# Strided attention of group A: queries and keys copied by ScalarE into neighbouring columns

## The chip, the core and the metric

The kernel runs on one core of a Trainium2 chip. The core has TensorE (PE in the profile, with PEld for its loads of stationary operands), VectorE (DVE), ScalarE (ACT), GpSimd (POOL) and SyncE (SP, which issues the DMAs here). Each engine works through its own instructions in the order in which they were written; semaphores order the engines among each other. The metric is device time in microseconds (us) of one launch, the median of several runs.

## What is computed

One decoder layer over 2048 tokens of width 1024. One projection feeds four groups of four heads (A to D), each with its own kind of attention, and a last projection `w_out` adds the gated outputs to the input. The change is in group A, dilated attention: each head attends three times with 128 queries to a block, with token strides 1, 4 and 16, and the three results are merged by their softmax denominators.

```python
DILATED_CONFIGS = ((128, 1), (512, 4), (2048, 16))

def dilated_attention(q, k, v, table_h):
    b, nh, s, dh = q.shape
    outs, lses = [], []
    for window, rate in DILATED_CONFIGS:
        fold = lambda t: t.reshape(b, nh, s // rate, rate, dh).transpose(0, 3, 1, 2, 4).reshape(b * rate, nh, s // rate, dh)
        o, lse = banded_attention(fold(q), fold(k), fold(v), table_h, window // rate, dist_scale=rate)
        ...
    wts = jax.nn.softmax(jnp.stack(lses, axis=0), axis=0)
    return jnp.sum(wts[..., None] * jnp.stack(outs, axis=0), axis=0).astype(q.dtype)
```

With stride 16 each of the 16 residue classes has 128 tokens, one block, so a block of queries sees its own block of keys alone. With stride 4 each of the 4 classes has 4 blocks, and a block sees its own and the one before it, except the first.

## The kernel before

The program goes through groups C, D, then A and B together, and the output projection. A Python planner writes it: it keeps a clock of its own for each engine (`T`), adds an estimated duration at each operation (`op`), and issues next whatever its clocks call ready. What comes out is one fixed order for each engine; on the chip nothing is reordered.

`group_ab` has 48 units of group A and 16 of group B. Units 0 to 31 are the strided ones (`make_a`, list `ORDER`): for each head four units of stride 16, then four of stride 4, each with four query blocks. Units 32 to 47 are the stride-1 units (`make_a1`), which alternate with the 16 units of group B (`make_b`). A unit runs like this:

- scores (`a_unit`, L1639): two matmuls a query block, since keys come as a rounded part and a remainder; eight a unit, into two PSUM tiles `s`. In a stride-16 unit all move 128 columns; in a stride-4 unit two move 128 and six 256.
- VectorE adds the bias and takes the row maximum (L1644, L1649); ScalarE takes exp and row sums (L1655).
- PE turns the weights (L393), ScalarE copies them rounded (`ph`, L399), VectorE makes the remainder (`pl`, L403), PE multiplies with the values (L422), ScalarE takes the result out of PSUM (`ot`, L371), PE turns it back (L435), and VectorE alone (L439) or ScalarE and VectorE (L442, L444) add its halves.

A head's queries and keys lie in SBUF by token: 2048 neighbouring columns of 4 bytes, in `wb` for even heads, in `AQ` and `keys` for odd ones. Before the change the strided units let the matmuls pick every 4th or 16th column, both for the stationary operand (queries) and for the moving one (keys). `make_a`'s `setup` also loads the next head, the bias rows and, at the end of the strided units, the first tiles of the stride-1 units (`a_more`) and of group B (`b_more`).

When nothing of a unit is ready for PE, the planner takes a step of the output projection (`out_proj`; three matmuls of 512 columns at L2148). 24 such matmuls are one job, a block of 128 rows, with one tanh (L2096) and one rounding copy (L2116) on ScalarE, four turns on PE (L2112), and on VectorE one product (L2100), one remainder (L2122) and two additions (L2154). The first 16 jobs (384 matmuls) need groups C and D; the other 16 need A and B of their rows, so the first of them waits for the first four stride-1 units.

## Time and profile before

| | us |
|---|---|
| median of 3 runs | 1802.55 (1792.04 to 1805.48) |
| the profiled execution, its own time | 1795.48 |
| its span, first to last instruction | 1793.7 |
| PE busy | 1721.8 (96%) |
| VectorE busy | 1330.1 (74%) |
| ScalarE busy | 1073.2 (60%) |

The profile is of one execution. Busy shares are means over stages with different limits; a PE that counts as busy need not run at its peak, since a matmul's end is modelled. In the trace the strided scores run from 1364.8 to 1504.5 us, the stride-1 units and group B up to about 1743 us, and then only output projection is left. The granted TensorE clock was 0.984 of full speed over the span.

### The profile page before, as it was taken

What the parts mean: (1) busy time and instruction counts of PE and PEld (TensorE: products, weight loads), DVE (VectorE), ACT (ScalarE), POOL (GpSimd) and SP (SyncE); (2) the same over time, 40 slices, a digit from 0 to 9 for tenths busy, and PEclk for the clock granted to TensorE, in tenths of its full rate; (3) what the DMA queues carried; (4) which work ended last, traced back from release to release, by engine and by line L of the source; (5) the groups of instructions that cost most, each with busy time, mean ns of one, the idle gap of its engine ahead of it and who ended that gap; (6) DMA issues with size and microseconds to landing.
All of it is one profiled execution on the core that took longest, in us unless ns stands there. A gap on an engine that the chain in (4) does not pass through costs nothing.

```text
span 1793.7 us, 31779 instructions
## 1 busy us (share of the span) xinstructions
PE 1721.8 (96%) x10035; PEld 1507.1 (84%) x10035; DVE 1330.1 (74%) x4072; ACT 1073.2 (60%) x2588; POOL 688.6 (38%) x841
## 2 busy tenths in 40 slices
PE   7989999999998999899989999999989999899999
PEld 5878878788787888789878789999869999788987
DVE  5446778998899996688476778887166777788873
ACT  4345556666675764567466566776256776467651
POOL 4666563544453654112344532223511121433231
PEclk9999999999999999999988999999999999999999
DMA  7763555334446325731484422323375768999986
GB/s 243 232 206 108 173 169 165 99 115 140 115 141 195 113 79 163 202 119 66 135 271 142 149 64 85 118 56 95 121 226 173 228 202 268 284 309 324 298 262 221
DMA packets 283480, 308.24 MB, mean 172 GB/s; under 512 B 80256, under 2 KB 201216, under 8 KB 282640
## 3 DMA queue, kind: packets, MB, share of 16 engines
q1 hardware_dynamic: 283312, 306.21, 55.5%
q8 instruction: 80, 1.31, 0.3%
q14 instruction: 88, 0.72, 0.1%
HBM read 219.47 MB, written 86.92 MB: 171 GB/s over the span
## 4 chain that ended last, share of the span: by engine, by line
PE 49%; DVE 3%; DMA 2%; issue 1%; POOL 1%; SPq 1%; ACT 1%; DVEq 0%; ACTq 0%; POOLq 0%
PE j L833 12%; PE o L422 9%; PE j L2148 8%; PE pt L393 7%; PE s L943 4%; PE s L1639 4%; PE pt L435 2%; PE s L1329 1%; PE s L1428 1%; SPq L156 1%; PE pt L2112 1%; PE s L1941 1%; DVE pl L403 0%; DMA BQ<-tqB 0%; DVE prow L945 0%
## 5 line engine op out<-in xcount | busy, mean ns | idle before, releaser
L833 PE MATMUL j<-wb,xh 128*128 128x512 f32 (+2 forms) x2048 | 619.6, 383 | 12.8 <-ACT wb L618 7.8
L833 PEld LDWEIGHTS j<-wb,xh 128*128 128x128 f32 x2048 | 372.2, 191 | 59.2 <-POOL xh L571 7.7
L833 PE MATMUL j<-wb,xl 128*128 128x512 f32 (+2 forms) x1024 | 386.4, 377 | 0.9 <-POOL xl L577 0.9
L399 ACT ACTIVATE ph<-pt 128x512 fp32r<-128x512 f32 (+4 forms) x486 | 265.4, 575 | 128.2 <-PE pt L393 121.3
L403 DVE TENSOR_TENSOR pl<-pt,ph 128x512 fp32r<-128x512 f32 (+4 forms) x486 | 311.4, 658 | 37.4 <-ACT ph L399 37.0
L833 PEld LDWEIGHTS j<-wb,xl 128*128 128x128 f32 x1024 | 194.6, 190 | 27.2 <-POOL xl L577 2.2
L679 POOL TENSOR_TENSOR ss<-ss,expo 128x6 f32<-128x6 f32 (+2 forms) x64 | 117.1, 1830 | 214.2 <-DVE ss L677 202.9
L577 POOL TENSOR_TENSOR xl<-xt,xh 128x512 fp32r<-128x512 f32 x112 | 150.1, 1340 | 9.3
L371 ACT ACTIVATE ot<-o 128x512 f32<-128x512 f32 (+1 forms) x160 | 81.5, 509 | 101.2 <-PE o L422 100.7
L943 PE MATMUL s<-keys,Q 128*128 128x512 f32 (+3 forms) x320 | 113.1, 400 | 11.8 <-DVE mx L945 6.9
L571 POOL TENSOR_SCALAR xh<-xt 128x512 fp32r<-128x512 f32 x128 | 84.5, 660 | 76.7 <-DMA xt<-in_xt_dram 48.0
L2102 POOL TENSOR_TENSOR xt<-xt,sq 128x512 f32<-128x512 f32 x32 | 41.6, 1299 | 184.6 <-DVE sq L2100 58.4
L660 ACT ACTIVATE stqk<-j 128x512 f32<-128x512 f32 x64 | 38.3, 598 | 122.8 <-PE j L833 122.7
L945 DVE CUSTOM_DVE_ANT_0 prow<-s,Hs 128x512 f32<-128x512 f32 (+3 forms) x160 | 94.3, 605 | 20.8 <-PE s L943 14.2
L674 DVE TENSOR_REDUCE ss<-sq 128x6 f32<-128x384 f32 (+2 forms) x64 | 39.4, 615 | 93.7 <-ACT sq L664 93.5
L1059 DVE SCALAR_TENSOR_TENSOR pa<-pb,ra,pa 128x1024 f32<-128x1024 f32 (+4 forms) x96 | 104.2, 1112 | 2.3
L945 DVE CUSTOM_DVE_ANT_0 pa<-s,H 128x512 f32<-128x512 f32 (+3 forms) x160 | 93.6, 604 | 14.1 <-PE s L943 12.1
L1655 ACT ACTIVATE ap<-ap,AO 128x128 f32<-128x128 f32 (+1 forms) x192 | 86.4, 454 | 24.0 <-DVE AO L1649 23.8
L945 DVE CUSTOM_DVE_ANT_0 pb<-s,H 128x512 f32<-128x512 f32 (+3 forms) x160 | 92.8, 603 | 4.1 <-PE s L943 3.2
L435 PE MATMUL pt<-ident,ot 128*128 128x128 f32 x512 | 86.7, 283 | 4.0 <-DVE pl L403 2.0
L1043 ACT ACTIVATE pa<-pa,nm 128x128 f32<-128x128 f32 (+7 forms) x64 | 76.9, 1202 | 22.1 <-DVE nm L951 21.7
L1523 ACT ACTIVATE prow<-prow,nm 128x128 f32<-128x128 f32 (+7 forms) x64 | 76.9, 1202 | 17.5 <-DVE nm L951 16.5
(265 smaller groups left out, 4206.3 us busy)
## 6 DMA issues: line engine op xcount, KB each, us to landing
xt<-in_xt_dram SPq DMA_DIRECT2D x128, 256.0 KB, 3.5
xr<-in_x_dram SPq DMA_DIRECT2D x16, 512.0 KB, 5.6
Q<-tqC SPq DMA_DIRECT2D x64, 128.0 KB, 3.3
DQ<-tqD SPq DMA_DIRECT2D x16, 512.0 KB, 4.8
raw<-gate_d SPq DMA_DIRECT2D x32, 256.0 KB, 4.4
stqk<-in_x_dram SPq DMA_DIRECT2D x32, 256.0 KB, 5.0
acc_d<-stqk SPq DMA_DIRECT2D x32, 256.0 KB, 4.4
stqk<-acc_d SPq DMA_DIRECT2D x32, 256.0 KB, 4.3
```

The costliest lines, as they stand in the source:

```text
L393: PE.transpose(ps[:rows, x * 128:(x + 1) * 128], src(), ident)
L399: A.activation(ph[:rows, :n], ps[:rows, :n], AF.Copy)
L403: V.tensor_tensor(pl[:rows, :n], ps[:rows, :n], ph[:rows, :n], op=OP.subtract)
L422: PE.matmul(u["po"][:, c0:c0 + wd], lhsT=lhsT(), rhs=x[:rows, col:col + wd], start=u["k"] == 1, stop=u["k"] == total, skip_group_check=True)
L435: PE.transpose(ps[:, i * 128:(i + 1) * 128], ot[:, i * 128:(i + 1) * 128], ident)
L577: G.tensor_tensor(l, xt, h, op=OP.subtract)
L679: G.tensor_tensor(ss[:, :nh], ss[:, :nh], expo[:, :nh], op=OP.pow)
L833: PE.matmul(ps[:, :n], lhsT=xx[:, ks], rhs=W[k][ww][:, lo:hi], start=(k == 0 and i == 0), stop=(k == KT - 1 and i == 2))
L943: PE.matmul(ps[:, :n], lhsT=q(), rhs=k[:, k0:k0 + n], start=(i == 0), stop=(i == np_ - 1))
L945: V.tensor_tensor_reduce(st["row"][:, k0:k0 + n], ps[:, :n], rev(H, t * 128 + 127 - k0, n), 1.0, LOW, OP.add, OP.max, st["mx"][:, ci:ci + 1])
L1059: V.scalar_tensor_tensor(rows[i][:, k0:k0 + n], part[i][:, k0:k0 + n], ra[:, 1:2], rows[i][:, k0:k0 + n], op0=OP.mult, op1=OP.add)
L2148: PE.matmul(ps, lhsT=xx[:, ks], rhs=OW[half, (k, c)][ww], start=(x == 0 and k == 0 and i == 0), stop=(x == len(halves) - 1 and k == 3 and ...
```

## The change

Two new tiles `AC`, each 128 partitions by 3 times 512 columns, are used in turn by the strided units. A new function `gather(n)` lets ScalarE copy a unit's 512 queries into the first third of its tile, in neighbouring columns; for stride 4 two more copies bring its 512 keys (rounded part and remainder) into the other thirds. The copies still read every 4th or 16th column. Stride-16 units keep reading their keys in place, with stride. The copies of unit n+1 are put off to 3 us (of the planner's clock) after unit n's setup, and a unit's scores wait for its own copies (`cready`). In all there are 16 + 16 * 3 = 64 copies of 128x512.

Three things go with it: the planner no longer counts strided scores as slower than others; the third part of the `AC` tiles takes the place of group B's query tile `BQ`, and the first two parts that of the last two tiles of output weights (`ow`); so `b_more`, which loads group B's first two units, moves from the setup of unit 28 to that of unit 32.

```diff
                     for x in range(2):
                         PE.matmul(ps[:, s0:s0 + n], lhsT=qs(j), rhs=ks(x, j, prevs[j]), start=(x == 0), stop=(x == 1))
-                        e = op("PE", mm(n) if r == 1 else max(217.0, 0.92 * n)) + 60.0
+                        e = op("PE", mm(n)) + 60.0
...
+        AC = [as_.tile([128, 3, 512], F32R, name="AC%d" % i) for i in range(2)]
+        cready = {}
+
+        def gather(n):
+            h, r, q0 = ORDER[n]
+            Q, K = QK[h % 2]
+            C = AC[n % 2]
+            for i, src in enumerate((Q,) if r == 16 else (Q, K[:, 0], K[:, 1])):
+                src = src.rearrange("p (c r) -> p r c", r=r)
+                if r == 16:
+                    A.activation(C[:, i].rearrange("p (j c) -> p j c", j=4), src[:, q0:q0 + 4], AF.Copy)
+                else:
+                    A.activation(C[:, i], src[:, q0 // 4], AF.Copy)
+                cready[n] = op("ACT", av(512), aready[h])
...
+                if n == 0:
+                    defer(aready[0], lambda: gather(0))
+                if n + 1 < len(ORDER):
+                    defer(max(T["PE"] + 3000.0, aready.get(ORDER[n + 1][0], 0.0)), lambda: gather(n + 1))
...
-                if n == len(ORDER) - 4:
-                    b_more()
...
             def source():
-                Q, K = QK[h % 2]
-
-                def cols(j, i0, n):
-                    rho, i = divmod(q0 + j, nb)
-                    c0 = rho + r * 128 * (i - i0)
-                    return slice(c0, c0 + (n - 1) * r + 1, r)
-                return (lambda j: Q[:, cols(j, 0, 128)]), (lambda x, j, p: K[:, x, cols(j, p, 128 * (1 + p))]), Hs[h, r]
+                C, K = AC[n % 2], QK[h % 2][1]
+                if r == 16:
+                    ks = lambda x, j, p: K[:, x, q0 + j::r]
+                else:
+                    ks = lambda x, j, p: C[:, 1 + x, (j - p) * 128:(j + 1) * 128]
+                return (lambda j: C[:, 0, j * 128:(j + 1) * 128]), ks, Hs[h, r]
...
-            u = a_unit(r, q0, setup, room, lambda: max(at("s"), aready[h]), source,
+            u = a_unit(r, q0, setup, room, lambda: max(at("s"), cready.get(n, INF)), source,
...
-                    parts += [as_.tile([128, 1024], F32R, name="ow%d" % i) for i in range(2)]
+                    parts += [t[:, 0:2].rearrange("p i c -> p (i c)") for t in AC]
+                    b_more()
...
-            Qb = as_.tile([128, 2, 256], F32R, name="BQ", bufs=2)
+            Qb = AC[hd[1] % 2][:, 2].rearrange("p (j c) -> p j c", j=2)
```

How the order moves, at three places. The first is ScalarE in the stride-4 units of head 0 (units 4 to 7). Before (`ap` are the weights, `pt` turned weights, `o` a unit's result):

```order
L1655 ACTIVATE ap,AO<-ap,AO 128x128
L1655 ACTIVATE ap,AO<-ap,AO 128x256
L399 ACTIVATE ph<-pt 128x512
L1655 ACTIVATE ap,AO<-ap,AO 128x256 x2
L371 ACTIVATE ot<-o 128x512
L1655 ACTIVATE ap,AO<-ap,AO 128x128
L1655 ACTIVATE ap,AO<-ap,AO 128x256
L399 ACTIVATE ph<-pt 128x384
```

ScalarE at the same place in the changed kernel; the lines below the change stand 16 to 18 higher in its file, so L2114 is the tanh of L2096:

```order
L1695 ACTIVATE AC_17188<-wb 128x512 x3
L1655 ACTIVATE ap,AO<-ap,AO 128x128
L1655 ACTIVATE ap,AO<-ap,AO 128x256
L399 ACTIVATE ph<-pt 128x512
L1655 ACTIVATE ap,AO<-ap,AO 128x256 x2
L2114 ACTIVATE sq<-raw 128x512
L371 ACTIVATE ot<-o 128x512
L1695 ACTIVATE AC_17187<-wb 128x512 x3
```

Three copies of the next unit now stand ahead of each stride-4 unit's exponentials, in the one queue of ScalarE.

The second place is PE at the last stride-4 unit of head 0 (unit 7). Before:

```order
L393 MATMUL pt<-ident,ap 128x128 x4
L1639 MATMUL s<-wb 128x128 x2
L1639 MATMUL s<-wb 128x256 x6
L422 MATMUL o<-ph,tl 128x256
L422 MATMUL o<-pl,tl 128x256
```

PE at unit 7 in the changed kernel; L2166 is the output projection of L2148:

```order
L393 MATMUL pt<-ident,ap 128x128 x4
L1639 MATMUL s<-AC_17188 128x128 x2
L1639 MATMUL s<-AC_17188 128x256 x6
L2166 MATMUL j<-wb,xh 128x512 x2
L2166 MATMUL j<-wb,xl 128x512
L2166 MATMUL j<-wb,xh 128x512 x2
L2166 MATMUL j<-wb,xl 128x512
L2166 MATMUL j<-wb,xh 128x512 x2
L2166 MATMUL j<-wb,xl 128x512
L2166 MATMUL j<-wb,xh 128x512 x2
L2166 MATMUL j<-wb,xl 128x512
L435 MATMUL pt<-ident,ot 128x128 x4
```

Matmuls of the output projection have moved in between the units. Counted over PE's whole order, the number of them ahead of the first score of each unit:

| PE's output projection (L2148, now L2166) ahead of | before | changed |
|---|---|---|
| unit 0 | 42 | 45 |
| units 1 to 27 (strided) | 21 | 171 |
| units 28 to 31 (strided) | 51 | 72 |
| units 32 to 35 (stride 1, with group B) | 120 | 96 |
| units 36 to 39 | 99 | 12 |
| units 40 to 47 | 207 | 171 |
| the end | 228 | 201 |

Along with them six more roundings and six more tanhs stand on ScalarE between unit 0 and the exponentials of unit 27, and seven additions of halves (L442) have moved from ScalarE to VectorE's L439.

The third place is SP's queue where group B's first loads are issued. Before (`AO<-o` is part of the merge of the last head, `raw<-in_w_out` an output weight):

```order
L156 DMA BQ<-tqB 128x2x256
L156 DMA BK<-tkB 64x2x256 x2
L156 DMA BV<-vvB 128x2x128
L156 DMA BQ<-tqB 128x2x256
L156 DMA BK<-tkB 64x2x256 x2
L156 DMA BV<-vvB 128x2x128
L156 DMA AO<-o_114 128x4x264
L156 DMA raw<-in_w_out_dram 128x512 x2
```

SP in the changed kernel, where they now stand behind that merge load and one more job of the output projection:

```order
L156 DMA AO<-o_114 128x4x264
L156 DMA xt<-yC 128x256
L156 DMA xt<-yD 128x256
L156 DMA raw<-gate_d 128x512
L156 DMA acc_d<-stqk 128x512
L156 DMA AC_17187<-tqB 128x2x256
L156 DMA BK<-tkB 64x2x256 x2
L156 DMA BV<-vvB 128x2x128
L156 DMA AC_17188<-tqB 128x2x256
```

The eight loads (of 256, 192 and 192 KB) now follow the last strided scores, since they overwrite a third of the tiles that these read; group B's first scores follow 75 matmuls later on PE, 18 of them of the output projection.

## Rows read from the trace of the kernel before

**Rows 1.** The page's first part: busy time of each engine, its share of the span, and its instructions.
```profile
PE 1721.8 (96%) x10035; PEld 1507.1 (84%) x10035; DVE 1330.1 (74%) x4072; ACT 1073.2 (60%) x2588; POOL 688.6 (38%) x841
```

**Rows 2.** Busy time by stretch, as the header line names the columns: units 0 to 27 (to the end of unit 27's scores), units 28 to 31, the passage to the stride-1 units, those units with group B, the end.
```profile
core 0: us, PE busy (x) PEld busy (x) DVE busy (x) ACT busy (x) POOL busy (x), PEclk, DMA share, GB/s
1364.80:1476.90 112.10, 111.09 (x697) 108.58 (x696) 83.66 (x352) 84.90 (x297) 16.71 (x11) 0.95 0.67 212
1476.90:1505.30 28.40, 28.19 (x154) 24.98 (x152) 17.72 (x57) 14.19 (x47) 7.63 (x6) 1.00 1.03 325
1505.30:1560.00 54.70, 48.98 (x304) 42.08 (x305) 45.67 (x138) 33.62 (x101) 17.24 (x17) 0.97 0.81 252
1560.00:1742.90 182.90, 181.54 (x1203) 161.16 (x1202) 152.92 (x535) 123.78 (x368) 57.63 (x82) 1.00 0.97 299
1742.90:1793.70 50.80, 47.01 (x217) 38.12 (x215) 20.95 (x37) 7.18 (x14) 10.30 (x10) 0.99 0.68 220
```

**Rows 3.** The chain of work that ended last, in order of time, (start us, us, what), eight score matmuls in a row each: twice of stride 4, twice of stride 16, once of stride 4, and the first stride-1 unit.
```profile
1382.28 1.99 PE s L1639 x8
1387.86 1.99 PE s L1639 x8
...
1392.15 1.73 PE s L1639 x8
1396.87 1.71 PE s L1639 x8
...
1454.44 1.86 PE s L1639 x8
...
1506.23 0.93 PE s L1639 x8
```

**Rows 4.** Loads of the stationary operand by the score line, least, median and greatest duration in ns: of units 24 to 27 (stride 16), and of units 32 and 33 (stride 1).
```profile
L1639 PEld LDWEIGHTS s<-keys,AQ x32: 295/310/310, 1463.5 to 1476.4; 128*128 128x128 f32 x32
...
L1639 PEld LDWEIGHTS s<-wb x16: 187/190/193, 1506.0 to 1517.0; 128*128 128x128 f32 x16
```

**Rows 5.** The same chain of work at the end, where PE does output projection alone.
```profile
1770.32 5.54 PE j L2148 x24
```

**Rows 6.** ScalarE's groups with each shape apart, over the whole span (count, then busy us and mean ns of one, then idle time before them and what ended it): the 512-column copies from PSUM to SBUF and the tanh from SBUF to SBUF, neighbouring columns all; and in units 0 to 27 the addition of halves.
```profile
L399 ACT ACTIVATE ph<-pt 128x512 fp32r<-128x512 f32 x388 | 220.3, 595 | 112.3 <-PE pt L393 105.4 <-PE j L833 1.9 <-DVE mx L945 1.1
L2096 ACT ACTIVATE sq<-raw 128x512 f32<-128x512 f32 x32 | 20.1, 628 | 6.5 <-DMA raw<-gate_d 4.0 <-POOL xt L2102 2.4
...
L442 ACT ACTIVATE AO<-pt 128x256 f32<-128x256 f32 x12 | 4.6, 382 | 0.3 <-PE pt L435 0.3
```

**Rows 7.** VectorE's groups in the same view: L775 adds a small table to a PSUM tile and writes its 512 results to SBUF with 32 columns (128 bytes) between neighbours; L403 has the same number of elements and writes neighbouring columns.
```profile
L403 DVE TENSOR_TENSOR pl<-pt,ph 128x512 fp32r<-128x512 f32 x388 | 258.9, 683 | 30.2 <-ACT ph L399 29.9
L775 DVE TENSOR_TENSOR sq<-pt,post 128x512 f32<-128x512 f32 x8 | 8.9, 1107 | 0.7 <-PE pt L741 0.7
```

**Rows 8.** Waits in the strided units (engine and line, what it waited for: us in total, times, longest).
```profile
ACT ot L371 <- PE o L422: 19.8, 21, 3.4
DVE ap L1644 <- PE s L1639: 19.4, 27, 2.4
ACT ap L1655 <- DVE AO L1649: 12.9, 11, 3.7
...
PEld s L1639 <- DVE amx L1644: 0.2, 1, 0.2
```

**Rows 9.** Four stride-1 units with their four of group B: busy time of all engines in the stretch, and then PE's time on the output projection alone (105 matmuls).
```profile
1645.30:1698.30 53.00, 53.00 (x355) 47.50 (x355) 46.91 (x163) 36.95 (x111) 17.45 (x25) 1.00 1.02 308
...
1645.30:1698.30 53.00, 28.87 (x105) 18.14 (x105) 1.00 1.02 308
```

**Rows 10.** VectorE's groups of the output projection, 1560 to 1742 us, shapes apart.
```profile
L2154 DVE TENSOR_TENSOR stqk<-j,stqk 128x512 f32<-128x512 f32 x29 | 19.9, 686 | 4.7 <-PE j L2148 3.6 <-DMA stqk<-acc_d 0.9
...
L2100 DVE SCALAR_TENSOR_TENSOR sq<-sq,raw 128x512 f32<-128x512 f32 x16 | 11.0, 690 | 0.0
L2122 DVE TENSOR_TENSOR xl<-pt,xh 128x512 fp32r<-128x512 f32 x16 | 10.9, 683 | 1.5 <-ACT xh L2116 1.5
```

**Rows 11.** The passage to the stride-1 units: two pieces of the chain of work, and group B's query loads among the DMA issues (count, KB each, median us from issue to landing).
```profile
1537.44 6.07 DMA wb<-vvA
...
1545.38 5.75 DMA stqk<-in_x_dram
...
BQ<-tqB SPq DMA_DIRECT2D x16, 256.0 KB, 6.4
```

## Prediction

> **What bounds the kernel now.** I read the page's busy times first: PE is busy for 96% of the span, the others for 74% at most [rows 1]. So a change pays if it takes work from PE and leaves PE fed. Then the table of stretches, since shares differ by stage [rows 2]. In the strided units PE is busy for 111.09 of 112.10 us, ScalarE for 84.90 and VectorE for 83.66; the reader is to see that PE ends nearly everything there, but that ScalarE has only 27 us to spare. The waits say the same from the other side: ScalarE and VectorE wait for PE (19.8 and 19.4 us), and PE's scores wait for them 0.2 us in all [rows 8]. Behind these units comes a passage in which PE is busy for 49.0 of 54.7 us, then stride-1 units and group B, where PE is full again, VectorE busy for 152.9 of 182.9 us and the DMA share 0.97, and last the output projection alone [rows 2].
>
> **What is removed: strided reading by PE.** In the chain of work, eight score matmuls in a row take 1.73 and 1.71 us with stride 16, 1.99, 1.99 and 1.86 us with stride 4, and 0.93 us for the first stride-1 unit, which has the shapes of a stride-4 unit and neighbouring columns [rows 3]. The loads of the stationary operand tell why: 310 ns with stride, 190 without [rows 4]. A stride-4 unit therefore saves 1.95 - 0.93 = 1.02 us.
>
> A stride-16 unit gets neighbouring queries, but its keys keep their stride. Bounds: nothing is saved (if the keys alone cost 1.72 us), or all but 0.93. The stride-4 rows decide: two of their eight matmuls move 128 columns (0.215 us each, as with stride 16), so the six of 256 strided columns take (1.95 - 0.43) / 6 = 0.253, half of which is 0.127 for 128 columns. Eight of these take 1.0 us, and a stride-16 unit saves 0.72.
>
> PE saves 16 * 1.02 + 16 * 0.72 = 27.8 us in all (16.3 by the lower bound), 23.8 of them in units 0 to 27 and 4.0 in units 28 to 31. If PE stayed the bound everywhere, the kernel would gain about that.
>
> **What is added: 64 copies on ScalarE.** No row of before shows ScalarE reading with stride. From below: 0.595 to 0.628 us, what 512 neighbouring elements take it [rows 6]. From above: VectorE writes 512 elements 128 bytes apart in 1107 ns and neighbouring ones in 683 [rows 7], 0.42 us more, which is 0.83 ns an element. Put on the 0.628 that gives 1.05 us. I take the upper end. The row is of another engine, and of a write; but PE's two strided reads also take nearly twice their time (0.253 against about 0.116 us for 256 columns, 310 against 190 ns a load), so three ports out of three slow down, each by its own pace.
>
> [...]
>
> ScalarE in units 0 to 27: 84.90 us now, plus 55 copies (the order has 55 ahead of unit 27's exponentials) at 1.05 = 57.8, plus six tanhs and six roundings of the output projection that move in, 6 * 0.628 + 6 * 0.595 = 7.3, less seven additions of halves, 7 * 0.38 = 2.7: 147.3 us.
>
> PE in the same units: 112.1 - 23.8 + 150 more matmuls of the output projection at 5.54 / 24 = 0.231 us [rows 5], 34.7, gives 123.0 us. So ScalarE becomes the bound of these units. It can't be busy all the time: its queue is fixed, and the three copies of the next unit stand ahead of a unit's exponentials, behind which wait VectorE's and PE's next steps. I take a share of 95%, between 100% and 85%, below PE's 99% in an order that fitted it: 147.3 / 0.95 = 155 us.
>
> Units 28 to 31: PE 28.4 - 4.0 + 21 * 0.231 = 29.3 us; ScalarE 14.2 + 9 * 1.05 + 0.6 = 24.3. PE stays the bound, since a long run of output projection still stands ahead of unit 28. The strided units take 155 + 29.3 = 184 us in place of 140.5: **44 us more**.
>
> **What is moved: output projection.** 171 of its matmuls leave the stretches behind, 171 * 0.231 = **39.5 us less** there. That is only a gain as far as PE is the bound there. Four stride-1 units with four of group B take PE 53.0 - 105 * 0.231 = 28.7 us without the projection, and VectorE 46.91 less 105 / 24 jobs at 2 * 0.686 + 0.690 + 0.683 = 2.75 us, so 34.9 [rows 9, 10]. Units 36 to 39 now have 12 matmuls of the projection in place of 99: VectorE 34.9 + 1.4 = 36.3 us against PE's 28.7 + 2.8 = 31.5, and VectorE bounds them. PE then idles 5 us, 7 at 95%: I take **6 us more**. In units 40 to 47 (85 matmuls to four units) PE has 48.4 us and VectorE 44.7, so nothing is lost.
>
> Group B's first eight loads now stand behind the last strided scores, and SP's queue behind them. A query load takes 6.4 us to land [rows 11]. Its cover is the 75 matmuls ahead of group B's first scores, 18 * 0.231 + 57 * about 0.12 = 11 us. I cost it at nothing. Without that cover it costs what loads cost the passage now, pieces of about 6 us [rows 11]; that passage loses 5.7 us of PE already, and may as well lose less. The shared tiles cost nothing else: output weights reach them long after the last strided scores.
>
> **The sum.** 44 - 39.5 + 6 = +10 us. The profiled execution took 1795.5 us, so it would take 1806. It ran 7 us below the median of the three runs, 1802.55; on the median the forecast is **1813 us, 0.6% above before**. A change within 1%, 18 us, is about what a measurement of this kernel can't tell from none.
>
> **The rivals.** *The copies are short* (0.63 us): ScalarE needs 84.9 + 55 * 0.63 + 7.3 - 2.7 = 124 us in units 0 to 27 and PE 123. Two engines so evenly loaded wait for one another; at 97% the stretch takes 128 us, and the sum is 128 + 29.3 - 140.5 - 39.5 + 6 = -17 us: 1786. For it: PE's moving port gets a strided column every 0.253 / 256 = 0.99 ns, which would leave ScalarE little to wait for; against it, rows 4 and 7, where the slower ports slow down as well. [...]
>
> *ScalarE stalls in its fixed queue*, the rival on the slower side: long copies, and exponentials behind them that wait for VectorE's maxima, which now wait for late scores. The order was laid out with PE full, so each late copy stops PE with output projection queued behind the scores. At a share of 85% the stretch takes 147.3 / 0.85 = 173 us, 18 more: 1831. It decides (18 us above before) from a share of 90% down. For it: ScalarE already waits 12.9 us for the maxima [rows 8]; against it, PE has 32 us of slack then, and copies don't need the unit at hand.
>
> *The change does not shorten the scores of stride 16*, because their keys keep the stride: 11.5 us of PE are not saved. With long copies that changes nothing, as ScalarE is the bound; with short ones it takes the gain down to 5 us or so.
>
> **How the numbers follow.** Long copies at 90 to 100%: 0.56; the likeliest, 1813, with a range of its own from 1805 to 1821. Short ones: 0.24, around 1786, a little under half of it more than 18 us faster. ScalarE stalling below 90%: 0.20, 1821 to 1840. Faster by over 1%: 0.11; slower by over 1%: 0.18 and a little of the first case, 0.23; within: 0.66. The range leaves out 0.1 at each end: 1785, within the short copies, and 1830, within the stalls, which also covers 6 us more or less in the passage.
>
> **What would show it.** In the profile after: the copies' mean (1.05 or 0.63 us) decides most. Eight scores of a strided unit should take 0.93 to 1.0 us. ScalarE should be busy 90% or more in units 0 to 27, PE about 80%, with waits of PE's scores for the copies; the strided units should end some 44 us later than now, and about 34 us of that be back by the end of the stride-1 units and the projection behind them. PE should wait for VectorE in units 36 to 39. The forecast is wrong if copies are short, if PE is full in the strided units, or if the passage grows by more than 6 us.

## The result and the profile after

The changed kernel took **1817.12 us**, median of 6 runs (1814.91 to 1823.26), the kernel before in the same comparison 1799.96 us, median of 6 (1792.04 to 1805.48). The ratio is 1.0108, 95% interval 1.0083 to 1.0132. Its profiled execution has a span of 1813.1 us, against 1793.7 before.

The page's busy times [rows 1]:

```profile
PE 1708.4 (94%) x10035; PEld 1480.0 (82%) x10035; DVE 1333.1 (74%) x4072; ACT 1129.2 (62%) x2645; POOL 688.8 (38%) x841
```

PE is busy for 13 us less than before, and the span is 19 us longer: what PE saved, and more, has become idle time. Where, the table of stretches tells [rows 2]. I cut both kernels at the same events, the first scores of units 0, 28, 32, 36, 40, 44 and 47 and PE's last matmul. In a row stand the stretch in us, its length, and the busy times of PE, PEld, DVE, ACT and POOL with their instructions; then the granted clock (1.00 is full speed), the DMA share and GB/s. First the kernel before:

```profile
1364.76:1493.02 128.26, 127.17 (x789) 122.22 (x788) 91.96 (x367) 89.94 (x311) 23.06 (x15) 0.96 0.72 225
1493.02:1505.74 12.72, 12.59 (x67) 11.81 (x66) 9.86 (x43) 9.59 (x34) 1.28 (x1) 1.00 1.00 339
1505.74:1578.33 72.59, 66.36 (x416) 56.86 (x415) 58.53 (x180) 44.94 (x133) 22.52 (x24) 0.98 0.85 262
1578.33:1631.56 53.23, 53.08 (x354) 47.25 (x353) 43.79 (x162) 36.35 (x110) 16.87 (x24) 1.00 1.01 315
1631.56:1686.46 54.90, 54.46 (x368) 49.01 (x367) 47.78 (x165) 37.80 (x112) 17.30 (x25) 1.00 1.01 307
1686.46:1725.50 39.04, 38.78 (x259) 34.48 (x258) 34.14 (x121) 27.33 (x82) 12.23 (x19) 1.00 1.05 320
1725.50:1789.67 64.17, 64.17 (x330) 53.31 (x328) 34.18 (x82) 17.73 (x45) 16.26 (x18) 1.00 0.68 220
```

And the changed kernel:

```profile
1370.42:1531.88 161.46, 142.48 (x956) 123.21 (x957) 110.27 (x392) 144.93 (x372) 30.29 (x20) 0.99 0.74 233
1531.88:1550.54 18.66, 15.48 (x92) 12.54 (x91) 10.27 (x40) 16.82 (x38) 1.30 (x1) 1.00 0.95 309
1550.54:1609.21 58.67, 54.04 (x342) 46.44 (x340) 52.79 (x171) 38.54 (x119) 19.23 (x22) 0.97 0.79 247
1609.21:1658.75 49.54, 40.62 (x288) 35.10 (x289) 41.77 (x158) 36.91 (x117) 14.00 (x22) 1.00 0.87 267
1658.75:1714.25 55.50, 52.22 (x344) 46.58 (x343) 44.97 (x162) 36.67 (x114) 18.49 (x27) 0.97 0.97 285
1714.25:1750.85 36.60, 35.66 (x245) 31.36 (x244) 30.91 (x117) 26.77 (x82) 11.13 (x17) 1.00 0.94 299
1750.85:1809.15 58.30, 58.30 (x308) 49.06 (x306) 31.32 (x78) 18.59 (x47) 14.52 (x17) 1.00 0.74 242
```

The strided units (two upper rows) take 180.1 us in place of 141.0, 39.1 more; all behind them 258.6 in place of 283.9, 25.3 less; and unit 0 starts 5.7 us later. Together 19.5 us, the difference of the two ends. In units 0 to 27 ScalarE, busy for 89.9 us before, is now busy for 144.9 of 161.5. In units 36 to 39 PE idles 8.9 us (49.54 less 40.62), where it had idled 0.2.

The copies, as ScalarE's groups by line in the strided units (busy us, mean ns of one, idle before); L1693 is the copy with stride 16, L1695 the one with stride 4:

```profile
L1695 ACT ACTIVATE AC<-wb 128x512 fp32r<-128x512 f32 x24 | 25.4, 1135 | 0.0
L1695 ACT ACTIVATE AC<-keys 128x512 fp32r<-128x512 f32 x16 | 17.0, 1115 | 0.0
L1695 ACT ACTIVATE AC<-AQ 128x512 fp32r<-128x512 f32 x8 | 9.1, 1140 | 0.0
L1693 ACT ACTIVATE AC<-AQ 128x512 fp32r<-128x512 f32 x8 | 8.8, 1096 | 0.0
L1693 ACT ACTIVATE AC<-wb 128x512 fp32r<-128x512 f32 x8 | 8.8, 1095 | 3.5 <-DMA yD<-Os 3.5
```

A copy lasts 1.10 to 1.14 us, at either stride. In ScalarE's timeline three in a row fill 3.25 us:

```profile
1402.60 3.25 ACT L1695 ACTIVATE AC<-wb 128x512 fp32r<-128x512 f32 x3
```

The next one starts about 0.1 us before the last ends, so a copy occupies ScalarE for 1.03 us (mean of 26 starts in a row; with stride 16, 0.98 to the start of what follows). The loads of the stationary operand [rows 4], now from the copies (ns min/median/max), in stride-4 units and in stride-16 units of even heads:

```profile
L1639 PEld LDWEIGHTS s<-AC x128: 186/189/192, 1386.2 to 1548.8; 128*128 128x128 f32 x128
L1639 PEld LDWEIGHTS s<-wb,AC x64: 186/192/195, 1370.7 to 1469.8; 128*128 128x128 f32 x64
```

The waits [rows 8], between 1360 and 1550 us (us in total, times, longest):

```profile
PEld s L1639 <- ACT AC L1695: 13.6, 19, 0.9
PEld pt L435 <- ACT ot L371: 11.6, 13, 2.3
PE s L1639 <- ACT AC L1695: 8.5, 17, 0.7
PE pt L435 <- ACT ot L371: 7.8, 9, 1.9
ACT AC L1693 <- DMA yD<-Os: 3.5, 1, 3.5
```

PE waits for ScalarE, for its copies and for results (`ot`) that stand behind copies in its queue. The last line is the first copy: it waits for group D's outputs to be stored, since its tile lies where they were.

In units 36 to 39 (1609 to 1659 us) PE waits mostly for VectorE's remainders:

```profile
PE o L422 <- DVE pl L403: 4.9, 4, 2.5
PE s L1959 <- DMA BK<-tkB: 1.3, 2, 0.6
PE pt L435 <- ACT ot L371: 1.1, 3, 0.5
```

### The profile page after: what moved, and what is told of

Read it like the earlier page. It is cut to its first block, busy times and chain, and to the rows that moved or that the text cites. A ratio compares the mean times of both kernels' runs of the same rounds, so it can differ in the third digit from the quotient of the medians.

```text
span 1813.1 us, 31851 instructions
## 1 busy us (share of the span) xinstructions
PE 1708.4 (94%) x10035; PEld 1480.0 (82%) x10035; DVE 1333.1 (74%) x4072; ACT 1129.2 (62%) x2645; POOL 688.8 (38%) x841
## 5 line engine op out<-in xcount | busy, mean ns | idle before, releaser
L833 PE MATMUL j<-wb,xh 128*128 128x512 f32 (+2 forms) x2048 | 621.4, 384 | 13.2 <-ACT wb L618 7.5
L403 DVE TENSOR_TENSOR pl<-pt,ph 128x512 fp32r<-128x512 f32 (+4 forms) x486 | 311.7, 659 | 45.2 <-ACT ph L399 44.8
L435 PE MATMUL pt<-ident,ot 128*128 128x128 f32 x512 | 87.0, 283 | 13.3 <-ACT ot L371 10.6
L435 PEld LDWEIGHTS pt<-ident,ot 128*128 128x128 f32 x512 | 61.0, 144 | 34.2 <-ACT ot L371 24.2
```

The source lines that it names most:

```text
L403: V.tensor_tensor(pl[:rows, :n], ps[:rows, :n], ph[:rows, :n], op=OP.subtract)
L435: PE.transpose(ps[:, i * 128:(i + 1) * 128], ot[:, i * 128:(i + 1) * 128], ident)
L833: PE.matmul(ps[:, :n], lhsT=xx[:, ks], rhs=W[k][ww][:, lo:hi], start=(k == 0 and i == 0), stop=(k == KT - 1 and i == 2))
```

## The experiments

They run from the copies to the units behind them, and then to kernels with other copies. The table has for each kernel how many matmuls of the output projection stand between the first scores of units 0 and 28, 28 and 36, 36 and 40 (from the order of the program), then from the profiled execution the start of unit 0, the length of the strided units and of all behind them to PE's last matmul, PE's idle time in both, and the ratio of medians to the kernel before on the same chip.

| kernel | projection | unit 0 at | units 0-31 | from 32 | PE idle | ratio (95%) |
|---|---|---|---|---|---|---|
| before | 69, 141, 108 | 1364.8 | 141.0 | 283.9 | 1.2 + 7.1 | |
| changed | 213, 126, 30 | 1370.4 | 180.1 | 258.6 | 22.2 + 17.8 | 1.0108 (1.0083-1.0132) |
| e1 neighbours | 213, 126, 30 | 1372.3 | 156.5 | 260.1 | 7.1 + 18.1 | 0.9973 (0.9951-0.9994) |
| e2 stride 16 only | 144, 147, 93 | 1370.8 | 151.5 | 272.6 | 4.3 + 13.2 | 1.0029 (1.0005-1.0053) |
| e3 before, late loads | 69, 135, 117 | 1369.0 | 142.8 | 289.4 | 1.2 + 10.4 | 1.0026 (1.0001-1.0051) |
| e4 unit 0 in place | 240, 102, 42 | 1375.2 | 185.8 | 267.5 | 19.1 + 26.1 | 1.0165 (1.0110-1.0220) |
| e5 true price | 336, 0, 30 | 1376.5 | 183.4 | 263.9 | 7.1 + 33.3 | 1.0153 (1.0113-1.0193) |
| e6 keys by GpSimd | 237, 99, 42 | 1376.6 | 161.3 | 262.4 | 5.5 + 22.6 | 1.0039 (1.0013-1.0065) |
| e7 held back | 177, 132, 66 | 1374.9 | 177.9 | 274.7 | 24.4 + 22.1 | 1.0176 (1.0146-1.0206) |
| e10 stores by GpSimd | 213, 126, 30 | 1367.7 | 182.3 | 257.1 | 20.3 + 15.4 | 1.0103 (1.0073-1.0132) |
| e11 late reloads | 213, 126, 3 | 1368.2 | 182.5 | 277.0 | 19.2 + 26.5 | 1.0190 (1.0169-1.0211) |
| e12 all by GpSimd | 243, 96, 30 | 1368.2 | 161.4 | 271.0 | 3.8 + 25.3 | 1.0041 (1.0021-1.0061) |
| e13 e12, held | 66, 150, 102 | 1368.1 | 148.0 | 283.7 | 19.7 + 9.1 | 1.0062 (1.0033-1.0092) |
| e14 e6, held | 150, 114, 102 | 1371.6 | 162.1 | 268.7 | 15.7 + 12.6 | 1.0010 (0.9993-1.0026) |

Unit 0's start moves by some us between kernels with the same code ahead of it (1370.4 us in the changed kernel, 1367.7 in e10); only the part shown below belongs to the change.

**e1, copies of neighbouring columns.** Every copy reads 512 neighbouring columns, so the scores are those of other queries and keys; all else is the changed kernel.

```diff
-                src = src.rearrange("p (c r) -> p r c", r=r)
-                    A.activation(C[:, i].rearrange("p (j c) -> p j c", j=4), src[:, q0:q0 + 4], AF.Copy)
+                    A.activation(C[:, i], src[:, q0 * 128:q0 * 128 + 512], AF.Copy)
...
-                    A.activation(C[:, i], src[:, q0 // 4], AF.Copy)
+                    A.activation(C[:, i], src[:, q0 * 128:q0 * 128 + 512], AF.Copy)
```

Expected:

> The changed kernel, but each copy reads 512 neighbouring columns in place of every 4th or 16th, so that the scores of the strided units are those of other queries and keys; instructions and order are the same. Theory A (ScalarE bounds the strided units because its copies read with stride): a copy takes 0.63 us in place of 1.06 to 1.14, ScalarE has 64 * 0.48 = 31 us less to do, the strided units take 157 us in place of 179, PE is full in them again, and the time falls by 15 to 22 us, to 1795 to 1802. Rival B (the loss comes from the order: output projection taken early, loads of group B late): a copy's length matters little, the strided units may shorten but the time gained is waited away behind them, and the time stays within 6 us of 1817.

Measured: 1796.45 us, median. ScalarE's groups, and the row of units 0 to 27:

```profile
L1694 ACT ACTIVATE AC<-wb 128x512 fp32r<-128x512 f32 x24 | 13.4, 629 | 0.0
L1694 ACT ACTIVATE AC<-keys 128x512 fp32r<-128x512 f32 x16 | 9.2, 624 | 0.0
```

```profile
1372.30:1513.30 141.00, 135.24 (x956) 121.56 (x957) 111.01 (x392) 119.82 (x372) 30.49 (x20) 1.00 0.85 268
```

With the same order on every engine, the stride of the copies alone costs 23.6 us in the strided units (180.1 against 156.5) and nothing behind them (258.6 against 260.1). It also shows PE's gain: behind unit 0 PE is busy for 391.4 us, against 416.6 in the kernel before, 25.2 less (sums of such rows). Not all of this need come from the reads, since in units 0 to 27 the granted clock was 0.96 before and is 1.00 here.

**e2, copies in stride-16 units only.** Stride-4 units read in place, and group B's first loads stand at unit 28 again.

```diff
             h, r, q0 = ORDER[n]
+            if r == 4:
+                cready[n] = aready[h]
+                return
...
+                if n == len(ORDER) - 4:
+                    b_more()
...
-                    b_more()
```

Expected:

> Copies in the stride-16 units alone (16 copies of queries); stride-4 units read in place as before the change, and group B's first loads are issued at unit 28 again, since nothing but those loads uses the last third of the tiles. Theory A: ScalarE gets 16 * 1.1 = 18 us, has about 102 of 112 us in units 0 to 27 and does not become the bound, while PE saves 16 * 0.75 = 12 us; with 5 us lost ahead of unit 0, where the first copy waits, the kernel takes 1790 to 1796, 4 to 10 us less than before (1800). Rival B (any copies in ScalarE's queue ahead of exponentials stall the units): PE waits for copies here as well, and the time is 1800 or more.

Measured: 1806.26 us, 10 above theory A. The time lies in rival B's range, but not by its cause: ScalarE is no bound here (PE idles 4.3 us in the strided units), yet nothing is gained. 75 matmuls more stand in units 0 to 27, and behind unit 32 84 fewer (567 in place of 651): at 0.231 us they should give back 19.4 us there, and give back 11.3, though group B's first loads are as early as before.

**e3, the kernel before with group B's first loads at unit 32.**

```diff
-                if n == len(ORDER) - 4:
-                    b_more()
...
                     parts += [as_.tile([128, 1024], F32R, name="ow%d" % i) for i in range(2)]
+                    b_more()
```

Expected:

> The kernel before with one thing of the change alone: group B's first loads are issued at the setup of unit 32 in place of unit 28, with tiles of their own. Theory A (the late loads are covered by the 11 us of PE work ahead of group B's first scores): within 3 us of before, 1797 to 1803. Rival B (they are a main part of the 14 us that PE idles more behind the strided units): 1806 to 1812.

Measured: 1805.15 us, 4.7 us above before (interval 0.2 to 9.2), between the two expectations. The late loads seem to cost some 5 us, though the interval comes near to nothing. The order behind them moves a little too (129 matmuls in place of 135 in units 32 to 35), so the price is not of the loads alone.

**e4, unit 0 in place.** Unit 0 reads as before the change, so no copy waits ahead of it.

```diff
+            if n == 0:
+                cready[n] = aready[h]
+                return
```

Expected:

> The changed kernel, but unit 0 reads in place, without a copy, so that the first copy is that of unit 1. In the profile of the changed kernel the first copy began at 1369.6 us, after a wait for a DMA (a store of group D), and the first strided score 5.7 us later than before. Theory A (the tile of the copies lies on memory that group D's last store still reads, and PE has nothing else): unit 0 starts within 1 us of before (1364.8) and the time falls by 3 to 6 us, to 1811 to 1814. Rival B (the start is hidden, since ScalarE bounds the units behind it and catches up): unit 0 starts earlier, but the time stays within 2 us of 1817.

Measured: 1833.3 us, what neither theory expected. From the start of group D's last score to unit 0's first score 24.3 us pass (24.4 in the kernel before, 27.0 in the changed one), so the first copy costs 2.7 us. But with one copy fewer at the start the planner lays the projection out otherwise (240 in units 0 to 27), and PE idles 45 us behind unit 0 in place of 40. The ratio is 1.0165 against 1.0108, some 10 us more than the changed kernel, though the two intervals overlap: an order that the planner arrives at by chance seems to outweigh the edit.

**e5, the planner knows the copies' price** (1040 ns; it counted 478).

```diff
-                cready[n] = op("ACT", av(512), aready[h])
+                cready[n] = op("ACT", 1040.0, aready[h])
```

Expected:

> The changed kernel, but the planner counts 1040 ns for a copy (it counted 478). It then lays 336 matmuls of the output projection between unit 0 and unit 28 (213 in the changed kernel), and none between units 28 and 36 (126). Theory (ScalarE's own work bounds the strided units, 1.1 us a copy): ScalarE gets five more jobs, 5 * 1.22 = 6 us, so units 0 to 27 take about 168 us in place of 161; units 28 to 35 are left without cover and give back less than the 29 us of matmuls that leave them. In all 1810 to 1824, no faster than the changed kernel. Rival (the planner's wrong price makes ScalarE stall, and a true price removes that): units 0 to 27 take less than 158 us and the whole less than 1806.

Measured: 1825.31 us, 1.3 above the theory's range. PE's idle time moves from the strided units (7.1 us) to the units behind (33.3 us). Waiting PE there cost more than was spared.

**e6, key copies on GpSimd.** ScalarE keeps the query copies.

```diff
-                else:
+                elif i == 0:
                     A.activation(C[:, i], src[:, q0 // 4], AF.Copy)
-                cready[n] = op("ACT", av(512), aready[h])
+                else:
+                    G.tensor_copy(C[:, i], src[:, q0 // 4])
+                    cready[n] = max(cready[n], op("POOL", 1900.0, aready[h]))
+                    continue
+                cready[n] = op("ACT", 1040.0, aready[h])
```

Expected:

> The changed kernel, but the 32 key copies of the stride-4 units go to GpSimd; ScalarE keeps the 32 query copies, counted as 1040 ns. Theory (the key copies on ScalarE are what bounds the strided units): ScalarE needs 84.9 + 28 * 1.1 + 8.5 - 2.7 = 122 us in units 0 to 27, PE 127, so they take about 131 us in place of 161, and the whole 1780 to 1792. Rival (such a copy takes GpSimd 3 us or more, or slows VectorE down): GpSimd or VectorE bounds the stride-4 units instead, at 7 us a unit or more, and the whole takes 1805 or more.

Measured: 1802.22 us. The theory's mechanism holds, its sum does not: units 0 to 27 take 145.8 us, PE busy for 140.8 of them. I had put PE's base at 112 us, a stretch that ends ahead of unit 28's run of projection; by the table's cuts it is 127. So these units win 15.7 us over the changed kernel. What the rival said of VectorE is seen as well (last section), but PE idles for 5.0 us only. Against before, units 0 to 31 still lose 20.3 us, for 195 more matmuls (45 us). Behind, 201 fewer matmuls (46 us) give back 21.5.

**e7, projection held back.** A limit on the projection's steps (of three matmuls) leaves 36 more matmuls for units 36 to 39.

```diff
                         def need():
                             prepare()
+                            if done >= OLIM[0]:
+                                return INF
...
                         yield need
+                        done += 1
...
+                OLIM[0] = 116 if m < 4 else 1000
...
+                OLIM[0] = 74 if n < len(ORDER) - 4 else 84
```

Expected:

> The changed kernel, but 36 matmuls of the output projection are held back from the strided units until unit 36, so that units 36 to 39 have 66 of them in place of 30. Theory (PE's idle 9 us in units 36 to 39 are a lack of cover for late loads and VectorE): the 8.3 us of matmuls fill them, these units take at most 3 us more, the strided units 2 us less, and the whole 1811 to 1818. Rival (nothing there waits for cover; the same idle time comes on top): units 36 to 39 take 8 us more and the whole 1821 to 1826.

Measured: 1829.05 us, worse than both expectations. Units 36 to 39 take 53.81 us, 4.3 more for 8.3 us of matmuls, so about half fell into idle time there. The strided units got 2.2 us shorter, as the theory had it, but every other stretch behind unit 32 got longer too (64.2 us in place of 58.7 in units 32 to 35), at a granted clock of 0.92 there.

**e10, stores by GpSimd.** Between 1590 and 1665 us of the changed kernel (units 34 to 40) SyncE's queue waits for GpSimd's results at the stores of merged outputs, with the next units' loads behind them:

```profile
SPq L156 <- POOL gst L448: 4.7, 1, 4.7
SPq L156 <- POOL AO L1901: 3.8, 2, 2.6
```

```diff
-    def mv(dst, src, after=0.0):
+    def mv(dst, src, after=0.0, by=None):
 
-        sy.dma_start(dst, src)
+        (by or sy).dma_start(dst, src)
...
-                    e = mv(dv(y_d["A"])[:, q0:q0 + 4, h * 64 - 64:h * 64 + 64], Y)
+                    e = mv(dv(y_d["A"])[:, q0:q0 + 4, h * 64 - 64:h * 64 + 64], Y, by=G)
```

(the store of yB likewise). Expected:

> The changed kernel, but the stores of group A's and group B's merged outputs (yA, yB) are issued by GpSimd, which makes them, and not by SyncE; every other engine's order is the same. Theory (in units 36 to 39 SyncE's queue waits about 9 us for GpSimd's results at these stores, with the next units' loads behind them, and PE waits for the loads): units 36 to 39 take 42 to 46 us in place of 49.5, and the whole 1807 to 1813. Rival (VectorE, busy for 84% there, bounds these units, as the prediction had it): they take 48 to 50 us and the whole 1815 to 1819.

Measured: 1815.87 us; units 36 to 39 take 51.02 us. The theory did not come true, but the experiment doesn't refute it, since the wait only moved: now SyncE waits for the store to land, at the load that brings yA back for the projection.

```profile
SPq L156 <- DMA yA<-AO: 11.0, 1, 11.0
```

**e11, that load comes later.** The projection's rows of groups A and B are loaded 6 us (of the planner's clock) after they are stored, behind the next units' loads.

```diff
-            return astored.get(t // 4 * 4, 0) == 4 and stored.get(t // 2 * 2, 0) == 2
+            if astored.get(t // 4 * 4, 0) < 4 or stored.get(t // 2 * 2, 0) < 2:
+                return False
+            return T["PE"] >= first.setdefault(t // 4, T["PE"]) + 6000
```

Expected:

> The changed kernel, but the output projection may load its rows of groups A and B only 6 us (of the planner's clock) after they are stored. Six loads that stood in SyncE's queue behind the first store yA and ahead of the next units' loads then stand behind those loads; units 36 to 39 have 3 matmuls of the projection in place of 30, 6.2 us less for PE. Theory (PE's idle 8.9 us in units 36 to 39 come from these loads, which wait for the store to land with the next units' queries and keys behind them): the idle time falls to 4 us or less, units 36 to 39 take 39 us or less in place of 49.5, and the whole 1809 to 1814. Rival (VectorE and the chain through it bound these units): PE idles 8 us or more there, they take 43 us or more, and the whole is 1815 to 1822.

Measured: 1833.03 us, worse than both expectations; most of the difference lies in the last stretch, 75.1 us in place of 58.3, where PE idles 7.5. Units 36 to 39, and PE's main wait there:

```profile
1611.52:1661.56 50.04, 37.87 (x239) 33.67 (x240) 34.56 (x143) 34.23 (x110) 12.39 (x18) 0.86 0.83 243
```

```profile
PE o L422 <- DVE pl L403: 6.0, 4, 2.5
```

SyncE's wait at the reload is gone, and with 27 matmuls fewer these units still take 50 us, with PE idle for 12. So neither that wait in SyncE's queue nor VectorE's load bounds them: VectorE is busy for 34.6 us of 50, 69%. A part of the 50 us goes with the granted clock, 0.86 (1.00 in the changed kernel): 27 matmuls fewer would leave PE 40.62 - 27 * 0.231 = 34.4 us of work, an estimate, and it is busy for 37.9.

**e12, all copies on GpSimd.**

```diff
-                    A.activation(C[:, i], src[:, q0 // 4], AF.Copy)
-                cready[n] = op("ACT", av(512), aready[h])
+                    G.tensor_copy(C[:, i], src[:, q0 // 4])
+                cready[n] = op("POOL", 1140.0, aready[h])
```

(the stride-16 copy likewise). Expected:

> The changed kernel, but GpSimd makes all 64 copies (counted as 1140 ns, what it took for a key copy). ScalarE is as free as before the change; PE bounds the strided units. Up to unit 28 PE has 127.2 - 25 + 174 * 0.231 = 142 us of work, up to unit 32 some 158 (141 before), and 192 fewer matmuls of the projection stand behind unit 32 than before. Theory (behind unit 32 a matmul that has left gives back only half of its time, since loads and VectorE bound those units then): from unit 32 to the end 258 to 264 us, as in the changed kernel, and the whole 1794 to 1804. Rival (it gives all of it back): 284 - 44 + 5 = 245 us, and the whole 1778 to 1786.

Measured: 1808.34 us, above the theory's range. ScalarE is free and PE full in the strided units (3.8 us idle), and behind unit 32 192 fewer matmuls (44 us) give back 12.9: less than even the theory said. The chain of work passes through PE here, so the shortened scores show whole, eight of stride 16 and eight of stride 4 [rows 3]:

```profile
1373.07 0.91 PE s L1639 x8
1395.28 0.93 PE s L1639 x8
```

**e13, the same, with the projection held** as in e7, to about the numbers that the kernel before has in each stretch.

```diff
+                OLIM[0] = 84 if m < 4 else 1000
...
+                OLIM[0] = 37 if n < len(ORDER) - 4 else 39
```

Expected:

> The same with all copies on GpSimd, but the output projection is held to about the number of matmuls that the kernel before has in each stretch (66 between units 0 and 28, 9 to unit 32, 141 to 36, 102 to 40). Theory (PE gains 25 us by the neighbouring columns, and loses them only by projection moved out of the units that need it): from unit 0 to 32 114 to 120 us (141 before), behind it 284 plus 5 for the late loads of group B, and the whole 1778 to 1790. Rival (VectorE, busy for 92 us there, and GpSimd, 86 us, stall PE when nothing of the projection fills the gaps): 130 us or more from unit 0 to 32, and the whole 1796 or more.

Measured: 1812.05 us. The strided units take 148.0 us, 7 more than before the change, though PE's scores are shortened by some 25 us (an estimate from the 25.2 of e1): what the rival said. Four pieces of 10 us of them:

```profile
1398.00:1408.00 10.00, 10.00 (x77) 9.12 (x76) 8.18 (x26) 7.81 (x25) 4.43 (x4) 1.00 0.79 245
1418.00:1428.00 10.00, 6.72 (x38) 5.86 (x36) 6.93 (x25) 4.10 (x13) 10.00 (x11) 0.83 0.86 272
1448.00:1458.00 10.00, 8.32 (x68) 7.54 (x68) 9.12 (x39) 8.94 (x34) 4.62 (x4) 1.00 0.86 273
1458.00:1468.00 10.00, 7.24 (x39) 6.67 (x40) 4.26 (x7) 3.76 (x9) 9.92 (x9) 0.66 0.43 141
```

PE is full in the first. In the second and the fourth GpSimd is full, with eight and five copies around the merging of a head's results in its queue. PE idles 3 us of 10, and the granted clock is 0.83 and 0.66. The gain is lost to such holes, in GpSimd's queue and, by the waits, behind VectorE's remainders too (8.6 us of PE's idle time between 1370 and 1540 us).

**e14, key copies on GpSimd, unit 0 in place, projection held** to 150, 114 and 102, by the theory that each stretch takes the longer of PE's work and of what the units need by themselves.

```diff
+                OLIM[0] = 100 if m < 4 else 1000
...
+                OLIM[0] = 64 if n < len(ORDER) - 4 else 68
```

Expected:

> Key copies on GpSimd, query copies on ScalarE, unit 0 read in place, and the output projection held to 150 matmuls between units 0 and 28, 15 to unit 32, 99 to 36, 102 to 40. Theory (each stretch takes the longer of PE's work and of what the units need by themselves, about 130 us for units 0 to 27 and 50 for four stride-1 units with four of group B; a matmul is free only until PE's work reaches that): units 0 to 27 take 125 to 132 us (PE's work is 127.2 - 25 + 81 * 0.231 = 121), 28 to 31 13 to 16, 32 to 35 57 to 60, 36 to 39 50 to 54, the rest 150 to 154; with no wait for the first copy the whole is 1778 to 1792, faster than before. Rival (the projection in the gaps doesn't decide; another order brings new gaps and low clock, as in the held kernels so far): PE idles 25 us or more behind unit 0, and the whole is 1797 or more.

Measured: 1805.25 us, ratio 1.0010 (0.9993 to 1.0026): what the rival said. Units 0 to 27 take 144.6 us where 125 to 132 were expected. PE idles for 13.9 of them, and is busy for 130.7 where 121 were expected, at a granted clock of 0.92:

```profile
1371.62:1516.21 144.59, 130.67 (x891) 119.26 (x890) 110.18 (x385) 118.91 (x342) 59.56 (x48) 0.92 0.77 244
```

No kernel here that computes the reference was faster than the one before.

## Why the prediction was right, and where it was off

It said 1813 us with no change over 1% as likeliest; 1817 came out, 1.1% slower, inside the range and just over the bound. The mechanism of the main term, ScalarE becoming the bound, is the one forecast; the change came out at nearly twice its forecast size, 17.2 us and not 10. Term by term:

- **PE's saving, 27.8 us.** About the size is shown: 25.2 us in e1, with the caveat on the clock; the eight scores at 0.91 and 0.93 us where 1.0 and 0.93 were forecast; loads at 189 to 192 ns. The rival that stride 16 wouldn't be shortened fell: with neighbouring queries alone, eight matmuls of 128 strided key columns take no longer (0.91 us) than eight stride-4 scores from copied keys (0.93). What the key copies of the stride-4 units save by themselves, two thirds of those units' copies, no run took apart.
- **The copies, 1.05 us.** 1.03 us of ScalarE each from one start to the next, 1.13 us long; neighbouring columns took 0.52 and 0.63 in e1. So a strided copy is longer by 0.50 us, where I had added 0.42 from VectorE's strided write. Strides of 16 and 64 bytes cost nearly the same, 1.13 and 1.10 us in length, 1.03 and 0.98 from start to start. Strided or not, a copy starts some 0.1 us before the one ahead of it ends.
- **ScalarE bounds the strided units, 184 us.** The bound is shown by e1, which takes time from ScalarE and keeps every order (156.5 us against 180.1), and borne out by e6 (161.3). To compare the sum, the changed kernel has to be cut where the prediction cut, at the end of unit 27's scores [rows 2]:

```profile
1370.42:1514.80 144.38, 127.51 (x868) 110.75 (x869) 100.84 (x369) 137.58 (x354) 22.14 (x15) 0.99 0.74 233
1514.80:1550.54 35.74, 30.46 (x180) 25.00 (x179) 19.69 (x64) 24.16 (x57) 9.45 (x6) 1.00 0.87 274
```

ScalarE's share was right, 95%. Its work was put too high, 147.3 us where 137.6 came out; at least in part this is because 358 of ScalarE's 371 instructions in units 0 to 27 start before the one ahead of them ends, by 0.10 us in the median (0.08 to 0.17), while the sum was made of lengths. So the stretch took 144.4 us and not 155, and PE was busy for 88% of it and not 80%. Units 28 to 31 took 35.7 us where 29.3 were forecast: PE was to stay full there, and idles 5.3 us, waiting mostly for copies and for results that ScalarE takes out. The two errors partly cancel, and the term came out as 39 us in place of 44.
- **The matmuls moved forward, -39.5 us.** PE's busy time behind unit 32 fell by 36.1 us (276.9 to 240.8). Some 2 of the missing 3.4 us agree with the granted clock, 0.97 in two stretches (3% of 58.7 and 55.5 us), where before it was 0.98 in one (2% of 72.6).
- **VectorE bounds units 36 to 39, +6 us.** This step failed in its cause. PE idles there about as forecast (8.9 us, 5 to 7 said), which is luck, since VectorE is busy for 84%, not 95%, and e11 took a sixth of its work away and won nothing. Four stride-1 units with four of group B take 50 us or more however little projection they have (3 matmuls in e11: 50.0 us; 30 in the changed kernel, e10 and e12: 49.5, 51.0 and 54.5; 66 in e7: 53.8; 108 before: 53.2), while PE's own work in them was worked out as 28.7 us. I had worked out the floor as the busiest engine's work over 95%, 38 us. By the waits it could be the units' own chain, from PE to VectorE, ScalarE and back, with few units under way. The changed kernel's chain of work in units 36 to 39 (start us, us, what) speaks for another cause as well: three loads of group B's keys make up 38% of it.

```profile
1607.45 5.73 DMA BK<-tkB
...
1635.41 6.20 DMA BK<-tkB
...
1654.35 6.83 DMA BK<-tkB
```

e10 and e11 changed what stands ahead of loads in SyncE's queue; no run gave these keys more tiles or an earlier load, so the cause stays open between the two. Idle time came up in units 40 to 46 too, 4.2 us in place of 0.7. In all the term is 10.7 us (17.8 less 7.1), not 6.
- **Late loads and shared tiles, nothing.** Both cost something: the loads about 5 us by e3, in part the same idle time as above, and the first copy, whose tile lay under group D's outputs, 2.7 us.

So the sum of +10 became 39.1 - 25.3 + 5.7 = 19.5 us between the two profiled executions, of which 3 us, the later start of unit 0 beyond the first copy's wait, are not the change; the medians differ by 17.2. That is nearly twice the forecast, and the range still covers it: the strided units cost 5 us less than forecast, the units behind gave back 8 less, and 5.7 came at the start, which was put at nothing.

The rival of short copies was in effect tried by e1: it came out at 1796, not at the 1786 forecast, because the units behind give back 10 us less than I had put in for both. The rival of a stalling ScalarE, with a share below 90% in the prediction's stretch, did not come: the share was 95%.

What the prediction missed as a whole is why no version gained. Every kernel that copies for all the strided units, or all but the first, shortens PE's reads, and loses the gain again: where the projection moves forward to fill it, the units behind run dry (e5, e6, e12), and where it is held back, the strided units do (e13), or both (e14). Behind unit 0 PE's idle time was 8.3 us before and 25 to 47 us in all of these. A part of the gain doesn't even show in PE's busy time, which fell by 25.2 us in e1 but by 13.3, 13.7 and 14.2 in e12, e13 and e14 and by 2.9 in e11, where the granted clock was lower in several stretches (0.86 to 0.95 in three of e11's first four). What sets the units' own pace, so that PE could use the gain, stays open; for the kernels in which GpSimd copies, the last section shows one more delay, of VectorE.

## What to carry to other kernels

Here copying data into a friendlier layout only moved the strided read to the engine that copies (ScalarE, 1.03 us a copy in place of 0.52); price the copy at its strided rate on that engine, and ask what that engine's share is in that stage. Where one engine is full only because independent work fills its gaps, time saved on it may be worth little until the gaps' own cause is gone (in e12 the 44 us of matmuls that had moved forward gave back 12.9): before counting a moved filler as a gain, ask what the stage takes without it, from its chain of dependent steps, loads included, and not from its busiest engine. In a planned order any edit of a price moves the filler, and the order alone was worth 12 us here (e7 against the changed kernel), so compare kernels with the same order where you can. And check a sum against the result in the stretches in which it was made.

## What the runs showed of the hardware

- ScalarE reads 512 fp32 columns 16 bytes apart at 1.03 us a copy, neighbouring ones at 0.52 (starts of copies in a row); the lengths are 1.13 us, 1.10 where they stand 64 bytes apart, and 0.63. GpSimd takes about the same for a strided copy (mean of one, 1165 ns):

```profile
L1697 POOL CAST AC<-wb 128x512 fp32r<-128x512 f32 x16 | 18.0, 1165 | 0.6 <-PE s L1639 0.6
```

- Some of VectorE's instructions took longer beside one of GpSimd, and ended just after it. In the strided units VectorE's 128x2 operation took 294 ns on average in the kernel before and 375 in e6, the projection's gate product 687 and 1097 ns; first the two rows of before, then those of e6, then one case in e6's timeline.

```profile
L1649 DVE TENSOR_SCALAR AO<-amx 128x2 f32<-128x2 f32 x63 | 18.5, 294 | 2.4
L2100 DVE SCALAR_TENSOR_TENSOR sq<-sq,raw 128x512 f32<-128x512 f32 x4 | 2.7, 687 | 0.0
```

```profile
L1649 DVE TENSOR_SCALAR AO<-amx 128x2 f32<-128x2 f32 x63 | 23.6, 375 | 2.2
L2122 DVE SCALAR_TENSOR_TENSOR sq<-sq,raw 128x512 f32<-128x512 f32 x10 | 11.0, 1097 | 0.2 <-ACT sq L2118 0.2
```

```profile
1474.32 3.83 POOL L1775 TENSOR_TENSOR AO<-AO,mg 128x1040 f32<-128x1040 f32 x2 [6.03 <-ACT mg L1772]
1474.44 1.84 DVE L1649 TENSOR_SCALAR AO<-amx 128x2 f32<-128x2 f32 x1
1476.31 0.51 ACT L1655 ACTIVATE ap<-ap,AO 128x256 f32<-128x256 f32 x1 [0.71 <-DVE AO L1649]
```

The means hide two kinds. Beside no GpSimd instruction the 128x2 operation took 168 to 171 ns in both kernels (53 of 63 in the kernel before, 42 of 63 in e6). Beside one it took up to 1.84 us, and each that took over 200 ns, 10 in the kernel before and 19 in e6, ended 23 to 29 ns after a GpSimd instruction did, as here, where the first of the two merging steps ends at 1476.26 us and VectorE at 1476.28. In e12, with all copies on GpSimd, there are 31 such. The remainders (L403), which read PSUM, took 678 ns beside GpSimd and 683 without in e6. So the copies on GpSimd are not free for VectorE: the longer operations add up to some 8 us in the kernel before, 13 in e6 and 15 in e12. What that costs the whole, no run shows.

- Idle time of PE cost twice in e13, where the granted clock was lower as well: it was 0.92 in units 0 to 27, where PE idled for 16.0 us of 130.1, and it was 1.00 in e1, where it idled for 5.8 of 141.0. PE was busy for 402.9 us behind unit 0, 11.5 more than in e1 for the same matmuls in another order. The two don't always go together: in the changed kernel PE idled for 19.0 us of the same units, at 0.99.
